# Batch normalisation over 64 tiles: stores moved to GpSimd's software queue in packets of eight rows, ScalarE computing most tiles

## The chip, the cores and the metric

One core of a Trainium2 chip runs the kernel. The metric is the device time of one execution in microseconds (us), the median over runs. A profile of one execution gives a span, from the first to the last instruction, and a record of each instruction and of each DMA packet.

## The reference

The input `x` has 32 images of 256 channels of 128 x 128 float32 values; each channel has a `gamma`, a `beta`, a running mean and a running variance. The result has the shape of `x`:

```python
mean = running_mean.reshape(1, -1, 1, 1)
var = running_var.reshape(1, -1, 1, 1)
return gamma * (x - mean) / np.sqrt(var + 1e-5) + beta
```

With `scale = gamma / sqrt(var + eps)` and `shift = beta - mean * scale`, every value needs one multiplication and one addition. 536.9 MB are read and 536.9 MB are written.

## The kernel before

The work is 64 tiles: an image's 256 channels are two blocks of 128, one channel on each partition, and a tile is 128 partitions of 16384 values (64 KB a row, 8.4 MB in all). Three buffers (`NBUF`) hold tiles; tile i lies in buffer i % 3, is computed in place and stored from there. Buffers are handed on by semaphores, which are written out by hand: `loaded[s]` and `stored[s]` count a buffer's loads and stores (16 for each DMA), `vdone` and `adone` count the parts done by VectorE and ScalarE.

At the start, SyncE (SP) issues the left half of tile 0, then the four small parameter loads, then the right half of tile 0. VectorE turns the parameters so that each partition has its channel's values, and works out `scale_t` and `shift_t`, with one square root on ScalarE.

Then the engines run over the tiles, each with an instruction order of its own.

- SP (L104) issues the load of tile i when the store of tile i - 3 is complete (L103), and also not before VectorE has done its first part of tile i - 1: a wait on `vdone` against 2 (i - 1) + 1. So one load is under way at a time.
- VectorE (`vector_part`, L132) computes columns 0 to 2560 (`STEP`) of a tile when it has landed, and then columns 2560 to 14336 (`VCOLS`).
- ScalarE (`scalar_part`, L143) computes the last 2048 columns. It waits for VectorE's two parts and, from tile 1 on, for the store of tile i - 1. Then it issues the store of tile i from its own queue (`store`, L156).
- The last tile is split anew: VectorE does 9216 columns (`VLAST`), ScalarE 7168 beside it.

At the end SP waits for all stores. `step` only chains the small parameter instructions to one another. GpSimd has no work but four small constants.

Of the kernel before, what the change touches and what calls it, by code (L numbers as in the profile page):

```python
# [7 lines left out]

NBUF = 3
PAD = 936  # L10


STEP = 2560
VCOLS = 14336
VLAST = 9216


@with_exitstack
def kernel(
    ctx: ExitStack,  # L20
    tc: tile.TileContext,
    x: bass.AP,
    gamma: bass.AP,
    beta: bass.AP,
    running_mean: bass.AP,
    running_var: bass.AP,
    out: bass.AP,
):
    nc = tc.nc
    eps = 1e-5  # L30
    f32 = mybir.dt.float32

    N, C, H, W = x.shape
    P = nc.NUM_PARTITIONS
    assert C % P == 0
    NCB = C // P
    HW = H * W
    NT = N * NCB
    B = 32
    NQ = P // B  # L40
    NE = 16
    NPAR = 4

    xr = x.rearrange("n (cb p) h w -> (n cb) p (h w)", p=P)
    outr = out.rearrange("n (cb p) h w -> (n cb) p (h w)", p=P)

    params = ctx.enter_context(tc.tile_pool(name="params", bufs=1))
    data = ctx.enter_context(tc.tile_pool(name="data", bufs=1))
    params.tile([P, PAD], f32, name="pad", tag="pad")
    bufs = [data.tile([P, HW], f32, name=f"t{s}", tag=f"t{s}") for s in range(NBUF)]  # L50
    rows = params.tile([B, NPAR * C], f32, name="rows", tag="rows")
    turned = params.tile([B, NPAR * C], f32, name="turned", tag="turned")
    par = params.tile([P, NPAR, NCB], f32, name="par", tag="par")
    eps_t = params.tile([P, 1], f32, name="eps_t", tag="eps")
    std_t = params.tile([P, NCB], f32, name="std_t", tag="std")
    rstd_t = params.tile([P, NCB], f32, name="rstd_t", tag="rstd")
    scale_t = params.tile([P, NCB], f32, name="scale_t", tag="scale")
    ms_t = params.tile([P, NCB], f32, name="ms_t", tag="ms")
    shift_t = params.tile([P, NCB], f32, name="shift_t", tag="shift")

    loaded = [tc.alloc_semaphore(f"loaded{s}") for s in range(NBUF)]
    stored = [tc.alloc_semaphore(f"stored{s}") for s in range(NBUF)]
    early = tc.alloc_semaphore("early")
    vdone = tc.alloc_semaphore("vdone")
    adone = tc.alloc_semaphore("adone")
    fetched = tc.alloc_semaphore("fetched")
    vec = tc.alloc_semaphore("vec")
    act = tc.alloc_semaphore("act")  # L70

    with tc.tile_critical():  # L72
        count = [0]

        def step(inst, sem=None, value=None):

            if sem is not None:
                inst._wait_ge(sem, value)
            elif count[0]:
                inst._wait_ge(vec, count[0])  # L80
            inst.then_inc(vec, 1)
            count[0] += 1
            return count[0]

        left, right = slice(0, HW // 2), slice(HW // 2, HW)
        last = NT - 1

        nc.sync.dma_start(out=bufs[0][:, left], in_=xr[0][:, left]).then_inc(early, 16)  # L90
        zeroed = step(nc.vector.memset(rows[:], 0.0))  # L91
        for r, ap in enumerate((running_var, gamma, beta, running_mean)):
            inst = nc.sync.dma_start(out=rows[0:NE, r * C : (r + 1) * C], in_=ap.partition_broadcast(NE))  # L93
            if r == 0:
                inst._wait_ge(vec, zeroed)
            inst.then_inc(fetched, 16)
        nc.sync.dma_start(out=bufs[0][:, right], in_=xr[0][:, right]).then_inc(loaded[0], 16)
        for i in range(1, NT):
            s, turn = i % NBUF, i // NBUF


            if turn:
                nc.sync.wait_ge(stored[s], 16 * turn)  # L103
            inst = nc.sync.dma_start(out=bufs[s][:], in_=xr[i]).then_inc(loaded[s], 16)  # L104
            if turn:
                inst._wait_ge(vdone, 2 * (i - 1) + 1)


        step(nc.vector.memset(eps_t[:], eps))  # L109
        step(nc.vector.transpose(out=turned[:], in_=rows[:]), fetched, 16 * NPAR)  # L110

        blocks = turned.rearrange("p (rc q b) -> p rc q b", q=NQ, b=B)
        flat = par.rearrange("p r cb -> p (r cb)")
        for q in range(NQ):
            placed = step(nc.vector.tensor_copy(out=flat[q * B : (q + 1) * B], in_=blocks[:, :, q, 0]))  # L115
        var_t, gamma_t, beta_t, mean_t = (par[:, r] for r in range(NPAR))
        nc.scalar.activation(  # L117
            out=std_t[:],
            in_=var_t,
            func=mybir.ActivationFunctionType.Sqrt,  # L120
            bias=eps_t[:],
            scale=1.0,
        )._wait_ge(vec, placed).then_inc(act, 1)
        step(nc.vector.reciprocal(out=rstd_t[:], in_=std_t[:]), act, 1)  # L124
        step(nc.vector.tensor_mul(out=scale_t[:], in0=gamma_t, in1=rstd_t[:]))  # L125
        step(nc.vector.tensor_mul(out=ms_t[:], in0=mean_t, in1=scale_t[:]))  # L126
        ready = step(nc.vector.tensor_sub(out=shift_t[:], in0=beta_t, in1=ms_t[:]))  # L127
        nc.vector.wait_ge(vec, ready)

        def vector_part(i, first, end):  # L130
            t, cb = bufs[i % NBUF], i % NCB
            return nc.vector.tensor_scalar(  # L132
                out=t[:, first:end],
                in0=t[:, first:end],
                scalar1=scale_t[:, cb : cb + 1],
                scalar2=shift_t[:, cb : cb + 1],
                op0=mybir.AluOpType.mult,
                op1=mybir.AluOpType.add,
            ).then_inc(vdone, 1)

        def scalar_part(i, first):
            t, cb = bufs[i % NBUF], i % NCB
            return nc.scalar.activation(  # L143
                out=t[:, first:],
                in_=t[:, first:],
                func=mybir.ActivationFunctionType.Identity,
                bias=shift_t[:, cb : cb + 1],
                scale=scale_t[:, cb : cb + 1],
            ).then_inc(adone, 1)

        def landed(i):
            return loaded[i % NBUF], 16 * (i // NBUF + 1)

        def store(i):
            s = i % NBUF
            nc.scalar.dma_start(out=outr[i], in_=bufs[s][:])._wait_ge(adone, i + 1).then_inc(stored[s], 16)  # L156

        vector_part(0, 0, HW // 2)._wait_ge(early, 16)
        vector_part(0, HW // 2, VCOLS)._wait_ge(*landed(0))
        for i in range(1, NT):  # L160
            vector_part(i, 0, STEP)._wait_ge(*landed(i))
            vector_part(i, STEP, VLAST if i == last else VCOLS)
        for i in range(last):
            nc.scalar.wait_ge(vdone, 2 * (i + 1))
            inst = scalar_part(i, VCOLS)
            if i:
                inst._wait_ge(stored[(i - 1) % NBUF], 16 * ((i - 1) // NBUF + 1))
            store(i)
        scalar_part(last, VLAST)._wait_ge(*landed(last))
        nc.scalar.wait_ge(vdone, 2 * NT)  # L170
        store(last)

        for s in range(NBUF):
            nc.sync.wait_ge(stored[s], 16 * ((NT - s + NBUF - 1) // NBUF))
# [30 lines left out]
```

## Time and profile before

| | us |
|---|---|
| median of 3 runs (2482.81 to 2484.91) | 2482.82 |
| span of the profiled execution | 2481.0 |
| VectorE busy in it | 508.8 |
| ScalarE busy in it | 139.8 |
| median time from issue to landing, load | 37.0 |
| median time from issue to landing, store | 36.5 |

How the profile is read: "busy" is the time in which an engine executes instructions; issuing a DMA is not counted. The DMA queues have rows of their own, with packets, megabytes and the share of the time of the core's 16 DMA engines that their packets took. q1 is SP's queue, q10 is ScalarE's. A window's "DMA share" is the mean busy share of the 16 engines, with packets counted where they start; the clock in it is TensorE's, which does nothing here. A timeline row has the start, the duration, the engine, the line and the operation; SPq and ACTq are the issuing instructions of SP and ScalarE.

### The profile page before, as it was taken

What the parts mean: (1) busy time and instruction counts of PE and PEld (TensorE: products, weight loads), DVE (VectorE), ACT (ScalarE), POOL (GpSimd) and SP (SyncE); (2) the same over time, 40 slices, a digit from 0 to 9 for tenths busy, and PEclk for the clock granted to TensorE, in tenths of its full rate; (3) what the DMA queues carried; (4) which work ended last, traced back from release to release, by engine and by line L of the source; (5) the groups of instructions that cost most, each with busy time, mean ns of one, the idle gap of its engine ahead of it and who ended that gap; (6) DMA issues with size and microseconds to landing.
All of it is one profiled execution on the core that took longest, in us unless ns stands there. A gap on an engine that the chain in (4) does not pass through costs nothing.

```text
span 2481.0 us, 516 instructions
## 1 busy us (share of the span) xinstructions
DVE 508.8 (21%) x139; ACT 139.8 (6%) x66; POOL 0.2 (0%) x4
## 2 busy tenths in 40 slices
DVE  2122121221212212122121221212212122121120
ACT  0000000000000000000000000000000000000001
POOL 0000000000000000000000000000000000000000
DMA  9999999999999999999999999999999999999999
GB/s 411 435 440 428 433 440 432 430 440 432 430 440 437 427 438 436 428 437 436 432 433 438 430 434 437 432 432 437 434 431 436 437 428 437 437 428 435 437 432 402
DMA packets 18708, 1073.85 MB, mean 433 GB/s; under 512 B 2128, under 2 KB 2192, under 8 KB 2192
## 3 DMA queue, kind: packets, MB, share of 16 engines
q1 hardware_dynamic: 9488, 536.94, 50.0%
q10 hardware_dynamic: 9216, 536.88, 49.9%
q14 instruction: 4, 0.03, 0.0%
HBM read 536.94 MB, written 536.87 MB: 433 GB/s over the span
## 4 chain that ended last, share of the span: by engine, by line
DMA 92%; DVE 4%; another core or an unknown queue 2%; ACT 0%; issue 0%; SPq 0%; DVEq 0%
DMA t<-in_x_dram 92%; DVE t L132 4%; ACT t L143 0%; SPq L93 0%; DVE rows L91 0%; DVE eps_t L109 0%; DVEq L200 0%; SPq L72 0%
## 5 line engine op out<-in xcount | busy, mean ns | idle before, releaser
L132 DVE TENSOR_SCALAR t<-t,scale_t,shift_t 128x11776 f32<-128x11776 f32 (+2 forms) x128 | 505.3, 3989 | 1928.8 <-DMA t<-in_x_dram 1928.7
L143 ACT ACTIVATE t<-t,shift_t,scale_t 128x2048 f32<-128x2048 f32 x64 | 138.2, 2159 | 2297.8 <-DMA out_dram<-t 2274.9
L110 DVE STREAM_TRANSPOSE turned<-rows 32x1024 f32<-32x1024 f32 x1 | 1.2, 1232 | 11.8 <-DMA rows<-in_running_mean_dram 11.8
L117 ACT ACT_TABLE_LOAD x1 | 1.3, 1283 | 0.9 <-SPq L72 0.9
L91 DVE MEMSET rows<- 32x1024 f32 x1 | 0.9, 912 | 1.2 <-SPq L72 1.2
L117 ACT ACTIVATE std_t<-par,eps_t 128x2 f32<-128x2 f32 x1 | 0.3, 295 | 14.0 <-DVE par L115 14.0
L115 DVE COPY par<-turned 32x8 f32<-32x8 f32 x4 | 0.6, 162 | 0.1
L124 DVE RECIPROCAL rstd_t<-std_t 128x2 f32<-128x2 f32 x1 | 0.2, 166 | 0.4 <-ACT std_t L117 0.4
L125 DVE TENSOR_TENSOR scale_t<-par,rstd_t 128x2 f32<-128x2 f32 x1 | 0.2, 162 | 0.0
L127 DVE TENSOR_TENSOR shift_t<-par,ms_t 128x2 f32<-128x2 f32 x1 | 0.2, 162 | 0.0
L126 DVE TENSOR_TENSOR ms_t<-par,scale_t 128x2 f32<-128x2 f32 x1 | 0.2, 160 | 0.0
L189 POOL MEMSET const-bfloat16-1.0<- 128x1 bf16 x1 | 0.1, 101 | 0.0
L189 POOL MEMSET const-uint8-127<- 128x1 uint8 x1 | 0.1, 101 | 0.0
L189 POOL MEMSET const-float32-0.0<- 128x1 f32 x1 | 0.1, 98 | 0.2 <-issue 0.2
L189 POOL MEMSET const-float32-1.0<- 128x1 f32 x1 | 0.1, 98 | 0.0
L109 DVE MEMSET eps_t<- 128x1 f32 x1 | 0.1, 59 | 0.1
## 6 DMA issues: line engine op xcount, KB each, us to landing
t<-in_x_dram SPq DMA_DIRECT2D x2, 4096.0 KB, 15.9
out_dram<-t ACTq DMA_DIRECT2D x64, 36.5
t<-in_x_dram SPq DMA_DIRECT2D x63, 37.0
rows<-in_running_var_dram SPq DMA_DIRECT2D x1, 16.0 KB, 11.1
rows<-in_gamma_dram SPq DMA_DIRECT2D x1, 16.0 KB, 10.9
rows<-in_beta_dram SPq DMA_DIRECT2D x1, 16.0 KB, 10.7
rows<-in_running_mean_dram SPq DMA_DIRECT2D x1, 16.0 KB, 10.6
```

What stands on the lines that cost most here:

```text
L91: zeroed = step(nc.vector.memset(rows[:], 0.0))
L109: step(nc.vector.memset(eps_t[:], eps))
L110: step(nc.vector.transpose(out=turned[:], in_=rows[:]), fetched, 16 * NPAR)
L115: placed = step(nc.vector.tensor_copy(out=flat[q * B : (q + 1) * B], in_=blocks[:, :, q, 0]))
L117: nc.scalar.activation(out=std_t[:], in_=var_t, func=mybir.ActivationFunctionType.Sqrt, bias=eps_t[:], scale=1.0,)._wait_ge(vec, placed).t ...
L124: step(nc.vector.reciprocal(out=rstd_t[:], in_=std_t[:]), act, 1)
L125: step(nc.vector.tensor_mul(out=scale_t[:], in0=gamma_t, in1=rstd_t[:]))
L126: step(nc.vector.tensor_mul(out=ms_t[:], in0=mean_t, in1=scale_t[:]))
L127: ready = step(nc.vector.tensor_sub(out=shift_t[:], in0=beta_t, in1=ms_t[:]))
L132: return nc.vector.tensor_scalar(out=t[:, first:end], in0=t[:, first:end], scalar1=scale_t[:, cb : cb + 1], scalar2=shift_t[:, cb : cb + 1 ...
L143: return nc.scalar.activation(out=t[:, first:], in_=t[:, first:], func=mybir.ActivationFunctionType.Identity, bias=shift_t[:, cb : cb + 1] ...
L189: nc = _bacc.Bacc("TRN2", target_bir_lowering=False, num_devices=1)
```

## The change

Stores are issued by GpSimd with `single_packet=True`, in tile order, each when ScalarE has counted its tile in `adone` (and for the first and the last tile when VectorE has done its part). The 128 rows of a store are spread over 16 DMA engines, eight rows in one packet for each. Loads stay on SP's queue: the first three are issued at once with semaphores of their own (`first`), and each later one waits for its buffer's store alone. ScalarE computes tiles 1 to 62 whole, one instruction of 16384 columns each; VectorE keeps the first half of tile 0 and 9216 columns of the last tile. ScalarE's wait for the previous store is gone, as is the load's wait for VectorE.

```diff
-STEP = 2560
-VCOLS = 14336
+NHEAD = 3
 VLAST = 9216
...
+    first = [tc.alloc_semaphore(f"first{s}") for s in range(NHEAD)]
...
-        nc.sync.dma_start(out=bufs[0][:, right], in_=xr[0][:, right]).then_inc(loaded[0], 16)
-        for i in range(1, NT):
-            s, turn = i % NBUF, i // NBUF
-            if turn:
-                nc.sync.wait_ge(stored[s], 16 * turn)
-            inst = nc.sync.dma_start(out=bufs[s][:], in_=xr[i]).then_inc(loaded[s], 16)
-            if turn:
-                inst._wait_ge(vdone, 2 * (i - 1) + 1)
+        nc.sync.dma_start(out=bufs[0][:, right], in_=xr[0][:, right]).then_inc(first[0], 16)
+        for i in range(1, NHEAD):
+            nc.sync.dma_start(out=bufs[i][:], in_=xr[i]).then_inc(first[i], 16)
+
+        def landed(i):
+            if i < NHEAD:
+                return first[i], 16
+            s = i % NBUF
+            before = 1 if s < NHEAD else 0
+            return loaded[s], 16 * (i // NBUF + 1 - before)
...
         nc.vector.wait_ge(vec, ready)
+        nc.scalar.wait_ge(vec, ready)
...
-        def landed(i):
-            return loaded[i % NBUF], 16 * (i // NBUF + 1)
-
-        def store(i):
+        vector_part(0, 0, HW // 2)._wait_ge(early, 16)
+        vector_part(last, 0, VLAST)._wait_ge(*landed(last))
+        scalar_part(0, HW // 2)._wait_ge(*landed(0))
+        for i in range(1, last):
+            scalar_part(i, 0)._wait_ge(*landed(i))
+        scalar_part(last, VLAST)._wait_ge(*landed(last))
+
+        for i in range(NHEAD, NT):
             s = i % NBUF
-            nc.scalar.dma_start(out=outr[i], in_=bufs[s][:])._wait_ge(adone, i + 1).then_inc(stored[s], 16)
-
-        vector_part(0, 0, HW // 2)._wait_ge(early, 16)
-        vector_part(0, HW // 2, VCOLS)._wait_ge(*landed(0))
-        for i in range(1, NT):
-            vector_part(i, 0, STEP)._wait_ge(*landed(i))
-            vector_part(i, STEP, VLAST if i == last else VCOLS)
-        for i in range(last):
-            nc.scalar.wait_ge(vdone, 2 * (i + 1))
-            inst = scalar_part(i, VCOLS)
-            if i:
-                inst._wait_ge(stored[(i - 1) % NBUF], 16 * ((i - 1) // NBUF + 1))
-            store(i)
-        scalar_part(last, VLAST)._wait_ge(*landed(last))
-        nc.scalar.wait_ge(vdone, 2 * NT)
-        store(last)
+            inst = nc.sync.dma_start(out=bufs[s][:], in_=xr[i])
+            if i >= NBUF:
+                inst._wait_ge(stored[s], 16 * (i // NBUF))
+            inst.then_inc(loaded[s], 16)
+        for i in range(NT):
+            if i in (0, last):
+                nc.gpsimd.wait_ge(vdone, 1 if i == 0 else 2)
+            nc.gpsimd.dma_start(out=outr[i], in_=bufs[i % NBUF][:], single_packet=True)._wait_ge(adone, i + 1).then_inc(
+                stored[i % NBUF], 16
+            )
```

## The prediction

> **What bounds the kernel now.** I read the page first: its queues, its busy times, its DMA issues.
>
> ```profile
> span 2481.0 us, 516 instructions
> DVE 508.8 (21%) x139; ACT 139.8 (6%) x66; POOL 0.2 (0%) x4
> ...
> q1 hardware_dynamic: 9488, 536.94, 50.0%
> q10 hardware_dynamic: 9216, 536.88, 49.9%
> ...
> out_dram<-t ACTq DMA_DIRECT2D x64, 36.5
> t<-in_x_dram SPq DMA_DIRECT2D x63, 37.0
> ```
>
> The two queues, loads (q1) and stores (q10), fill 50.0 + 49.9% of the time of the 16 DMA engines. VectorE is busy for 21%, ScalarE for 6%. So the bound is the time that packets take on the DMA engines, and a compute edit counts only where those engines run dry. Next, stretches of eight packet times (19.31 us, so that whole packets are counted), to see whether the mix of reads and writes matters.
>
> ```profile
> core 0: us, DVE busy (x) ACT busy (x) POOL busy (x), PEclk, DMA share, GB/s
> 2452.40:2471.71 19.31, 0.00 (x0) 0.00 (x1) 0.00 (x0) 1.00 1.00 434
> 34.00:53.31 19.31, 0.00 (x0) 0.00 (x0) 0.00 (x0) 1.00 1.00 434
> 1000.00:1386.24 386.24, 79.36 (x20) 20.93 (x10) 0.00 (x0) 1.00 1.00 434
> ...
> 5.00:24.31 19.31, 7.96 (x11) 0.29 (x1) 0.00 (x0) 1.00 1.02 433
> ```
>
> Row by row: stores alone 434 GB/s, loads and stores in turn 434, ten tiles of the middle 434, loads alone 433 (with the small parameter loads among them). The mix does not matter. The packet records say the same: a row of 64 KB takes 2418 ns in either queue, and one engine starts the next 2414 ns after the last; a packet of 32 KB takes 1213 ns. So 32 KB more cost 1205 ns, 64 KB cost 2410, and about 4 ns a packet are lost between packets. A tile is 8 rows on each engine, 8 x 2.414 = 19.3 us; load and store together 38.6 us, which is the spacing of the store issues (1003.58, 1042.18). The last view is the end of the timeline.
>
> ```profile
> 2433.65 0.34 ACTq L156 DMA_DIRECT2D out_dram<-t  x1
> 2446.04 6.36 ACT L143 ACTIVATE t<-t,shift_t,scale_t 128x7168 f32<-128x7168 f32 x1 [12.42 <-DMA t<-in_x_dram]
> 2446.04 5.27 DVE L132 TENSOR_SCALAR t<-t,scale_t,shift_t 128x2560 f32<-128x2560 f32 x2 [31.21 <-DMA t<-in_x_dram]
> 2452.43 0.34 ACTq L156 DMA_DIRECT2D out_dram<-t  x1
> ```
>
> The last tile lands at 2446.04 and takes 6.36 us of compute. The engines don't idle meanwhile: store 62, issued at 2433.65, is still being moved, and by the packet records store 63 follows it without a gap. That cover is what I watch below.
>
> **The change, part by part.** All sums are on the profiled execution: span 2481.0, of which the engines move data from 1.95 to 2479.36 (packet records). The median of the runs, 2482.82, lies 1.8 above the span; I add that at the end.
>
> *Compute.* ScalarE takes whole tiles. From the two widths in the groups, 2048 columns in 2092 ns and 7168 in 6362, a column costs 0.834 ns, so 16384 cost 2.09 + 14336 x 0.000834 = 14.05 us. 62 of them are 871 us, a third of the span, under 38.6 us of DMA time per tile. VectorE loses 126 of its 128 instructions; none was on the path. Price zero while the engines have other packets; the 14.05 us count only for when a store becomes ready. Tile 0's second half, 8192 columns, costs 2.09 + 6144 x 0.000834 = 7.2 us on ScalarE instead of 3.48 + 2.09 on both, so store 0 is some 2 us later, and with GpSimd's issue 4: hidden, for loads 1 and 2 (2 x 19.3 us from 23.4 on) are queued from the start.
>
> *Loads without the two gates.* Load i now waits for its slot's store alone, no longer for the previous tile's first vector step, and ScalarE's tiles no longer wait for the previous store. With three slots, one is loading, one is computed and stored, one is queued to load. Slot k is free again about 0.4 (landing to compute) + 14.05 + 2 (issue) + up to 5 (turn) + 19.3 + 2 = 43 us after load k landed; it is needed when load k+2 has ended, 77 us after. So 34 us are in hand, and the load queue never runs dry in the middle. Gain zero too, since the engines are already full at 434 GB/s.
>
> *Packets of eight rows.* 128 rows over 16 engines are 8 per engine. If the 4 ns are lost per packet, 7 x 4.2 ns x 64 stores = 1.9 us are saved; if they are lost per row, nothing. I take 1.9, since 32 KB and 64 KB packets carry the same excess over size. The engine takes turns between queues by packet: in the records of the middle, q1 and q10 alternate. So a store will hold its engine for 19.3 us while loads stand still, then loads run alone. By the windows neither direction alone is slower.
>
> *GpSimd issues the stores.* No GpSimd DMA is in this trace, so issue to first data is bounded by the nearest rows: the first load of all moves 1.0 us after its issue on SP; a store on ScalarE's queue at 1003.58, which had to await its turn, 3.5. [...]
>
> *What queues behind what.* GpSimd has nothing but stores on it, so a store that waits for ScalarE holds up only later stores. SP's next load waits for a store's completion with the 34 us in hand. A load's completion mark is a packet of its own and can be caught behind a store's 19.3 us packet; that delays ScalarE, again inside the 34 us.
>
> *The end.* Store 62 is ready 0.4 + 14.05 + 2.0 = 16.5 us after load 62 landed. Load 63 began when load 62 ended and has then done 6 to 7 of its 8 packets on each engine. The records show that a store waits 2.5 to 4.6 us more for its turn (3.5 to 5.6 us from issue, less the 1.0), so it starts 19.0 to 21.1 us after: about when the eighth packet is due. On whichever engine the store goes first, load 63's end, or its completion mark, comes only after the store. Then load 63 lands when store 62 is already over. Nothing is left to move while tile 63 is computed: 0.4 from the last data to compute, 6.36 of compute, 2.0 for GpSimd's issue: 8.8 us with idle DMA engines, where before there were none. Bounds: with 1.0 and 3.5 for the issue, 7.8 to 10.3.
>
> **Sum:** 2481.0 - 1.9 + 8.8 = 2487.9 span; with 1.8, **2489.7 us**. With the bounds, 2488.7 (or 2486.8 if GpSimd had no delay at all) to 2493.1 (no packet saving, late issue).
>
> [...]
>
> **The rivals.**
> 1. *The end stays covered.* If store 62 comes after load 63 has wholly ended, tile 63 is computed under it, and no engine idles. It decides at about 19.3 us from landing to the store's start on all engines, and I put that start at 19.0 to 21.1. But a store that misses load k+1 then runs in a pair with store k+1, and tile 63 must be the second of its pair; with tile 0 alone (its half tile is ready early) pairs are 1-2 to 61-62, and 63 is left over. For: the turn is close. Against: this parity. Time 2481.0 - 1.9 + 1.8 = 2480.9, no change. Chance 0.11.
> 2. *The packet stays one row.* If the flag does nothing here, loads and stores alternate as before, store 62 is stretched over 38.6 us and covers the end as it does now: 2482.8, no change. 9216 packets in the store queue would show it. Chance 0.11.
> 3. *The software queue is slower.* Each 1% on the stores is 64 x 19.3 x 0.01 = 12.4 us, undisguised, as the engines are the bound. The nearest bad row: the packets around the first store (28 to 34 us) took 2830 ns on average instead of 2418, once, 0.8 us per engine. If each store's start cost that, 64 x 0.8 = 51 us. In the middle none does. With 1% and the open end: 2502; with the 51 us, 2541. Chance 0.14.
> 4. *Faster.* At 2410 ns a row throughout, 1024 rows an engine need 2467.8; with 1.95 ahead and 1.6 behind the span is 2471.4, the time 2473.2. To gain over 5 us, half of what lies above that floor must go, and the 1.9 of the packets is not enough; the rest would have to come from the slow packets of the first 34 us (0.8 + 0.8 us per engine) and the 0.5 spread over later ones, with the end covered. Time about 2477. Chance 0.12.
>
> **How the numbers follow.** The forecast's case has 0.52. What a measurement can tell from no change is 0.2%, 5 us: 2477.9 to 2487.8. Of the forecast's case some 0.44 lies above 2487.8 and 0.08 below. Slower: 0.44 + 0.14 = 0.58. Same: 0.08 + 0.11 + 0.11 = 0.30. Faster 0.12. The range: below 2479 lies the fourth rival, 0.12; above 2500 more than half of the third, 0.08; so 2479 to 2500. The forecast's case alone is 2487 to 2493.
>
> **What would show it.** Right: a store queue of some 2048 packets (1024 of 512 KB and the marks); ScalarE tiles of 14.05 us; store issues 38.6 us apart on average; stores landing in about 25 us (2 + 3.5 for the turn + 19.3) instead of 36.5 and loads, issued early, in about 73 (3 x 38.6 - 43) instead of 37.0; after the last load lands, 8 to 9 us with no packets, then 19.3 us of store 63 alone. Wrong: DMA engines idle elsewhere, a stores-only stretch clearly under 434 GB/s, engines that end far apart, or store 62 still moving while tile 63 is computed.

## The result, and the profile after

Over 20 runs each, the changed kernel took 2495.57 us in the median (2485.83 to 2519.09), the kernel before 2483.8 (2482.39 to 2487.68): a ratio of 1.006, 95% interval 1.0039 to 1.008. It is slower by 0.6%. The median says less than the list: 9 of the 20 executions lie at 2485.8 to 2487.0, the other 11 anywhere from 2493.8 to 2519.1. The kernel before has no such second kind. I call them the low and the late executions. The profile below is of a low one (span 2484.1).

First its page: busy times, queues, issues to landing.

```profile
span 2484.1 us, 272 instructions
DVE 13.1 (1%) x13; ACT 885.6 (36%) x66; POOL 34.4 (1%) x68
...
q1 hardware_dynamic: 9488, 536.94, 49.9%
q0 software_dynamic: 9216, 536.88, 49.9%
...
out_dram<-t POOLq DMA_DIRECT2D x64, 46.3
t<-in_x_dram SPq DMA_DIRECT2D x63, 55.2
```

q0 is GpSimd's queue. It has 9216 packets, exactly as many as q10 had before: 8192 rows of 64 KB and 1024 completion marks. In the packet records of the middle the queues take turns on an engine after one row, at times two, so nothing held an engine for eight rows: the packets of eight rows that the title and the change speak of did not come about. Stores take 46.3 us to land, loads 55.2, for both queues now have work at nearly all times.

The windows of the same run: the middle, then the last tile's compute, then what follows the last row.

```profile
core 0: us, DVE busy (x) ACT busy (x) POOL busy (x), PEclk, DMA share, GB/s
1000.00:1386.24 386.24, 0.00 (x0) 140.40 (x10) 5.33 (x10) 1.00 1.00 434
2448.50:2455.20 6.70, 5.08 (x1) 6.36 (x1) 0.00 (x0) 1.00 0.90 391
...
2477.30:2484.10 6.80, 0.00 (x0) 0.00 (x0) 0.00 (x0) 1.00 0.00 1
```

The middle is as full as before, 434 GB/s. While the last tile is computed the engines are 90% busy: store 62 is still being moved. But 6.8 us pass after the last row, where the kernel before needed 1.6 (2479.36 to 2481.0). SP's own waits name the cause.

```profile
SPq L158 <- DMA out_dram<-t: 2367.0, 61, 69.4
...
SPq L70 <- POOLq L70: 5.1, 1, 5.1
```

When all stores have landed, SP waits 5.1 us for GpSimd. The instruction records have it as a DRAIN on GpSimd at the end of the block, 5292 ns long. So a low execution sums up as 2481.0 + 5.2 (end) - 2.1 (the last row ends at 2477.27 instead of 2479.36) = 2484.1. Of the 2.1, some 1.4 us per engine come from the end, where the engines finish within 0.6 us of one another instead of 2.6, and 0.6 from fewer slow rows.

### The profile page after: what moved, and what is told of

Its sections match the earlier page's. It is cut to its first block, busy times and chain, and to the rows that moved or that the text cites. A ratio compares the mean times of both kernels' runs of the same rounds, so it can differ in the third digit from the quotient of the medians.

```text
span 2484.1 us, 272 instructions
## 1 busy us (share of the span) xinstructions
DVE 13.1 (1%) x13; ACT 885.6 (36%) x66; POOL 34.4 (1%) x68
## 3 DMA queue, kind: packets, MB, share of 16 engines
q0 software_dynamic: 9216, 536.88, 49.9%
## 4 chain that ended last, share of the span: by engine, by line
another core or an unknown queue 61%; ACT 35%; DMA 2%; issue 0%; SPq 0%; DVE 0%; POOL 0%; DVEq 0%
ACT t L139 35%; DMA t<-in_x_dram 2%; SPq L89 0%; DVE rows L87 0%; POOL out_dram L165 0%; SPq L93 0%; DVE eps_t L105 0%; DVEq L196 0%; SPq L70 0%
## 5 line engine op out<-in xcount | busy, mean ns | idle before, releaser
L139 ACT ACTIVATE t<-t,shift_t,scale_t 128x16384 f32<-128x16384 f32 (+1 forms) x64 | 884.0, 13813 | 1554.3 <-DMA t<-in_x_dram 1554.3
L165 POOL DMA_DIRECT2D out_dram<-t x64 | 34.2, 535 | 2421.1 <-ACT t L139 2421.1
L128 DVE TENSOR_SCALAR t<-t,scale_t,shift_t 128x8192 f32<-128x8192 f32 (+1 forms) x2 | 9.6, 4813 | 2426.7 <-DMA t<-in_x_dram 2426.5
## 6 DMA issues: line engine op xcount, KB each, us to landing
out_dram<-t POOLq DMA_DIRECT2D x64, 46.3
t<-in_x_dram SPq DMA_DIRECT2D x63, 55.2
```

What stands on the lines that cost most here:

```text
L128: return nc.vector.tensor_scalar(out=t[:, first_col:end], in0=t[:, first_col:end], scalar1=scale_t[:, cb : cb + 1], scalar2=shift_t[:, cb ...
L139: return nc.scalar.activation(out=t[:, first_col:], in_=t[:, first_col:], func=mybir.ActivationFunctionType.Identity, bias=shift_t[:, cb : ...
L165: nc.gpsimd.dma_start(out=outr[i], in_=bufs[i % NBUF][:], single_packet=True)._wait_ge(adone, i + 1).then_inc(stored[i % NBUF], 16)
```

## The experiments

**1. The late executions, and what the flag does.** The changed kernel again, and the changed kernel without its flag:

```diff
-            nc.gpsimd.dma_start(out=outr[i], in_=bufs[i % NBUF][:], single_packet=True)._wait_ge(adone, i + 1).then_inc(
+            nc.gpsimd.dma_start(out=outr[i], in_=bufs[i % NBUF][:])._wait_ge(adone, i + 1).then_inc(
```

> The changed kernel as it is, to see whether one chip shows both kinds of execution: 9 of its 20 runs lay at 2485.8 to 2487.0 us, 11 between 2493.8 and 2519.1, and the profile is of the lowest. Theory A (the software queue has good and bad executions): both kinds among these runs, and a profile above 2490 us shows packets of over 2418 ns or gaps in the store queue. Theory B (the loads without gates slip into another order in some executions): both kinds too, but the packets stay at 2418 ns and the excess is time in which engines have no packet.

> The changed kernel with single_packet left out. The profile of the changed kernel shows 8192 store packets of 64 KB that take turns with the loads row by row, so by it the flag does nothing: 9216 store packets again, the same 5 us of GpSimd at the end, a span of about 2484 in the best execution, and the same spread. If the flag does act in a way the records do not show, and it makes the spread, all runs lie near 2486.

Both kinds showed in each, on one chip. e1_after_again: 6 of 12 runs at 2485.9 to 2486.3, 6 at 2499.5 to 2512.1. e2_no_flag: 5 of 12 at 2485.8 to 2486.7, 7 at 2496.8 to 2523.2; its queue has the same 9216 packets and its drain the same 5292 ns. So the flag does nothing that a packet count, a duration or a time shows.

The profile of e1_after_again caught a late execution. Its windows, an early stretch, a later one, and the compute of the last tile:

```profile
core 0 of [0], span 2510.4 us
...
300.00:1000.00 700.00, 0.00 (x0) 253.22 (x19) 9.59 (x18) 1.00 1.00 434
1200.00:2400.00 1200.00, 0.00 (x0) 424.41 (x31) 15.99 (x30) 1.00 1.00 429
2474.90:2484.00 9.10, 5.08 (x1) 6.36 (x1) 0.53 (x1) 1.00 0.39 166
```

It starts like a low one at 434 GB/s and falls to 429 after 1200 us, with the engines busy throughout (share 1.00): packets take longer. While tile 63 is computed the share is 0.39: here most engines have run out of work, the idle end that the prediction had put into every execution. By the packet records the last row ends 26.3 us later than in the low execution. What rows of 64 KB take beyond 2418 ns, called slow rows from here on, makes 18.2 us per engine instead of 0.7, and idle time 9.5 instead of 0.9. The two differences, 17.5 and 8.6, are nearly all of it. The idle time lies at the end: 9.2 us of it in the last 40 us before the last row ends, against 0.3 in the low execution. So this late execution is slow rows for two thirds and the open end for one third. Both queues have slow rows (11.0 us per engine in stores, 7.2 in loads). Theory A had expected them in the store queue, theory B no slow rows at all: neither was right on that.

**2. Software queue or missing gates?** Two kernels, each with one of the two. e3_act_queue is the changed kernel with its stores on ScalarE's hardware queue; e4_before_gpsimd is the kernel before with its stores on GpSimd:

```diff
 # e3_act_queue, against the changed kernel
             scalar_part(i, 0)._wait_ge(*landed(i))
+            nc.scalar.dma_start(out=outr[i], in_=bufs[i % NBUF][:])._wait_ge(adone, i + 1).then_inc(
+                stored[i % NBUF], 16
+            )
 ...
-            nc.gpsimd.dma_start(out=outr[i], in_=bufs[i % NBUF][:], single_packet=True) ...
 # e4_before_gpsimd, against the kernel before
-            nc.scalar.dma_start(out=outr[i], in_=bufs[s][:])._wait_ge(adone, i + 1).then_inc(stored[s], 16)
+            nc.gpsimd.dma_start(out=outr[i], in_=bufs[s][:], single_packet=True)._wait_ge(adone, i + 1).then_inc(stored[s], 16)
 ...
-        nc.scalar.wait_ge(vdone, 2 * NT)
+        nc.gpsimd.wait_ge(vdone, 2 * NT)
```

> The changed kernel with the stores on ScalarE's hardware queue, each right behind its tile's instruction; GpSimd issues nothing. It keeps the loads without gates and ScalarE's whole tiles. Theory A (everything comes from the software queue): no end of 5 us, no spread, 2480 to 2483 us in all runs, 0 to 3 below the kernel before. Theory B (the loads without gates make the spread): best runs at 2480 to 2483, others 8 to 33 us above.

> The kernel before with its stores issued by GpSimd with single_packet, all gates and VectorE's share kept. Theory A (software queue): 5 us more than before at the end in every run, 2488 us at best, and the spread of the changed kernel. Theory B (loads without gates): 2488 in all runs and no spread. [...]

This pair separates them. e3_act_queue has both kinds, 5 of 12 runs at 2481.0 to 2484.3 and 7 at 2492.9 to 2513.8, without any GpSimd DMA. e4_before_gpsimd has one kind, 2487.1 to 2489.9 in 11 runs; ratio to the kernel before 1.002 (1.0012 to 1.0029). So the late executions belong to the loads and tiles without gates, not to the software queue, which costs little but its drain: 5.6 us by the medians (2489.03 against 2483.42 on the same chip). The two kernels also differ in who computes the tiles; experiment 4 comes back to that. The page of e3_act_queue, a low execution:

```profile
span 2479.3 us, 269 instructions
...
q1 hardware_dynamic: 9488, 536.94, 50.0%
q10 hardware_dynamic: 9216, 536.88, 50.0%
```

At 2479.3 its span is 4.8 below the changed kernel's: the drain is gone, the even finish of the engines is kept. In e4_before_gpsimd stores take 36.2 us to land, against 36.5 on ScalarE's queue: neither VectorE's work nor GpSimd's issue costs anything here that can be seen.

**3. What the drain depends on.** Four kernels, each the kernel before with some work for GpSimd; `kept(i)` is the semaphore and count of store i, as software and hardware stores have semaphores of their own here:

```diff
 # e7_gpsimd_memset                # e8_gpsimd_one_dma: a 16 KB load on GpSimd in its place, awaited by SP at the end
+        nc.gpsimd.memset(spare[:], 0.0)
 # e9_last_on_gpsimd: soft(i) is i == NT - 1;  e10_first32_gpsimd: i < 32
+            queue = nc.gpsimd if soft(i) else nc.scalar
-            nc.scalar.dma_start(out=outr[i], in_=bufs[s][:])._wait_ge(adone, i + 1).then_inc(stored[s], 16)
+            queue.dma_start(out=outr[i], in_=bufs[s][:])._wait_ge(adone, i + 1).then_inc(kept(i)[0], 16)
 ... (the other waits on stored[...] become waits on kept(...))
```

> The kernel before plus one memset of 32 x 256 on GpSimd at the start, no DMA of GpSimd's: GpSimd then takes part in the drain at the end of the block. If the 5.3 us drain comes with any work of GpSimd: span 2486, time 2488. If it comes with the software queue: as before, 2482 to 2485.

> The kernel before plus one small load (16 KB) issued by GpSimd at the start, of data that nothing uses. If the drain at the end comes with the software queue, however little it moved: GpSimd's drain takes 5.3 us after the last store, span 2486, time 2488. If it grows with the 64 stores: under 1 us more than before.

> The kernel before with only the last store on GpSimd. One small GpSimd load at the start left a drain of 0.13 us, 64 stores one of 5.29. If the drain comes with a software DMA late in the kernel: 5.3 us again, span 2486. If it grows with the number of software DMAs: under 0.3 us, span 2481 to 2483.

> The kernel before with the first 32 stores on GpSimd, the rest on ScalarE's queue. If the drain grows with the number: about 2.7 us. If it comes with a software DMA late in the kernel: 0.1 us, as none is near the end. If it comes with any stores of that size: 5.3 us.

GpSimd's drain took 41 ns with the memset, 125 with the one load, 135 with the last store, 2669 with the first 32 stores, 5292 with 64. In these kernels it grows with the number of software DMAs, not with their bytes (a load of 16 KB and a store of 8.4 MB differ by 10 ns): (2669 - 135) / 31 = 82 ns for each from one DMA to 32, (5292 - 2669) / 32 = 82 ns for each from 32 to 64. The wait of SP in e10_first32_gpsimd, where GpSimd had issued nothing for the second half:

```profile
SPq L82 <- POOLq L82: 2.5, 1, 2.5
```

e7 and e8 are not to be told from the kernel before (ratios 1.0001, 0.9992 to 1.001, and 1.0004, 0.9994 to 1.0013). e9 and e10 ran once each (2483.56 and 2487.21 us), so for them the drain's own record counts and not the time. The last store on GpSimd in e9 landed 27.1 us after its issue, the same store on ScalarE's queue in the kernel before 27.3.

**4. Which gate.** One gate put back into e3_act_queue, and one gate taken from the kernel before:

```diff
 # e5_load_gate, against e3_act_queue
+            nc.sync.wait_ge(*landed(i - 1))
             inst = nc.sync.dma_start(out=bufs[s][:], in_=xr[i])
 # e6_store_gate, against e3_act_queue
+            nc.scalar.wait_ge(stored[(i - 1) % NBUF], 16 * ((i - 1) // NBUF + 1))
             scalar_part(i, 0)._wait_ge(*landed(i))
 # e11_before_no_load_gate, against the kernel before
-            if turn:
-                inst._wait_ge(vdone, 2 * (i - 1) + 1)
 # e12_before_no_store_gate, against the kernel before
-            if i:
-                inst._wait_ge(stored[(i - 1) % NBUF], 16 * ((i - 1) // NBUF + 1))
```

> The kernel with stores on ScalarE's hardware queue and ScalarE computing whole tiles (e3_act_queue), plus one gate: load i is issued only when load i - 1 has landed. Theory C (the engines fall out of step because a queue holds more than one load, and a load gate puts them in step again each tile): all runs at 2481 to 2484 us, none above 2488. Theory D (the store side sets it: stores of two tiles in flight): half of the runs 10 to 33 us above, as without the gate.

> The same kernel (e3_act_queue) with the other gate alone: ScalarE starts tile i only when the store of tile i - 1 is complete; loads as slots come free. Theory C (load gate): the spread stays, best runs 2481, others up to 2515. Theory D (store gate): all runs within 3 us. In both the engines stay busy in the middle, since a load or a store is always queued.

> The kernel before without the load gate (the wait on VectorE's first part of the previous tile); all else kept. Theory C (several loads in the queue let the engines fall out of step): a spread of 10 to 30 us above a best of 2481 to 2483. If the store gate alone keeps order: all runs within 5 us.

> The kernel before without the store gate (ScalarE's wait for the previous store); the load gate kept. Theory C: no spread, all runs within 5 us of 2483. If both gates are needed: a spread as large as the changed kernel's.

Measured, in us; the last two columns are per engine, from the packet records of each run's profile, and "slow rows" is again the time beyond 2418 ns:

| kernel | runs | last row ends | slow rows | idle |
|---|---|---|---|---|
| before (both gates) | 2482.0 to 2487.7 | 2479.4 | 1.3 | 2.4 |
| e11: store gate only | 2720.4 to 2729.7 | 2725.8 | 103.8 | 146.0 |
| e12: load gate only | 2553.1 to 2556.5 | 2551.5 | 61.7 | 14.0 |
| e3: no gate, whole tiles, low execution | 2481.0 to 2513.8 | 2477.1 | 0.7 | 0.6 |
| e5: e3 with a load gate | 2488.2 to 2492.6 | 2486.6 | 8.6 | 2.1 |
| e6: e3 with the store gate | 2728.3 to 2731.0 | 2727.0 | 114.0 | 137.2 |

I had forecast none of the large numbers; three of the four expectations were out by 70 to 250 us, and e5's by 4 to 8. In each row the added slow rows and idle time make up the distance from the kernel it was made from (e11: 102.5 + 143.6 = 246.1, against 246.4).

No kernel with a gate shows the two kinds in its 4 to 11 runs. e5 is the closest test: whole tiles on ScalarE as in e3_act_queue, one gate more, and its 6 runs lie within 4.4 us. So whole tiles alone do not make the late executions; a load gate ends them, but at 4 to 8 us above the level that had been expected. Two things stay untested here: e5 ran on another chip than e3_act_queue, and the kernel before was not tried with its own split of the tiles and neither gate.

How e11 loses its time can be read off. Its timeline, two of its windows and the wait of its loads; then, for comparison, the kernel before around the issue of a store (1003.58) and of a load (1017.59):

```profile
1018.66 7.93 DVE L130 TENSOR_SCALAR t<-t,scale_t,shift_t 128x2560 f32<-128x2560 f32 x2 [34.39 <-DMA t<-in_x_dram]
1021.06 84.77 SPq L104 DMA_DIRECT2D t<-in_x_dram  x3
1021.06 2.10 ACT L141 ACTIVATE t<-t,shift_t,scale_t 128x2048 f32<-128x2048 f32 x1 [40.24 <-DMA out_dram<-t]
1023.19 0.34 ACTq L154 DMA_DIRECT2D out_dram<-t  x1
```

```profile
core 0: us, DVE busy (x) ACT busy (x) POOL busy (x), PEclk, DMA share, GB/s
1017.00:1024.00 7.00, 5.34 (x2) 2.10 (x1) 0.00 (x0) 1.00 0.80 300
1024.00:1060.00 36.00, 2.59 (x1) 0.00 (x0) 0.00 (x0) 1.00 0.99 421
```

```profile
SPq L104 <- DMA out_dram<-t: 2615.0, 61, 67.0
```

```profile
core 0: us, DVE busy (x) ACT busy (x) POOL busy (x), PEclk, DMA share, GB/s
1001.00:1008.00 7.00, 0.00 (x0) 2.09 (x1) 0.00 (x0) 1.00 1.04 449
1015.00:1022.00 7.00, 6.05 (x2) 0.00 (x0) 0.00 (x0) 1.00 1.01 440
```

A load has landed at 1018.66, and at 1021.06 the store before it completes, which releases the next load and ScalarE's part at once. Load and store then set out together, take turns for 36 us and end together; both queues are empty at the same moment, and each of the 62 periods (42.1 us by the next issue) loses 143.6 / 62 = 2.3 us of idle time and 1.7 us in the first rows after it. The loads wait 2615.0 us in all, 42.9 each, for a store: tiles have landed one ahead, so the slot that a load needs is the one being stored. In the kernel before the engines are full at both issues. e6_store_gate gets there in another way: store i cannot be issued before 14.05 us of compute after store i - 1 has landed, and issue to landing is 28.3, so a period is 42.4 us instead of 38.6, whatever the loads do.

```profile
ACT t L139 <- DMA out_dram<-t: 1786.1, 62, 44.3
```

Those are ScalarE's waits in e6_store_gate, 28.8 us a tile, all on stores. So the two gates of the kernel before are a pair: together they keep a load's issue 14.0 us behind the store's (1017.59 and 1003.58 in the kernel before), so that one queue covers the other's gap; without the load gate 246 us are lost in the profiled execution, without the store gate 72. How the 72 us of e12 come about was not tested. The time between the two issues may matter: the store follows a load's issue by 8.5 us in e12 (1012.41 and 1020.87) and by 14.0 in e5 (2341.52 and 2355.55), which also has only a load gate and loses 9 us, not 72. Without both gates the low execution is tighter than with them (idle 0.6 instead of 2.4), but more than half of the executions are late.

## Why the prediction was right or wrong, point by point

The direction and the range held, and 0.6% is close to the forecast 0.3%. The mechanism did not hold, and the closeness is luck: the forecast added -1.9 and +8.8 us, a low execution is +5.2 - 2.1, the median over both kinds 11.8 above the kernel before. No low execution has the end that the forecast priced at 8.8 us, as far as profiled; the one late execution that was profiled has it. The two other costs that the runs show, the drain and the slow rows, were priced at nothing. One bound was also added up wrongly: without any delay of GpSimd the time by the forecast's own terms is 2489.7 - 2.0 = 2487.7, not 2486.8.

- *What bounds the kernel*, and that reads, writes and their mix go at one rate: right for before (433 and 434 GB/s in its windows); the mix in the middle of the low execution after has 434 GB/s.
- *Compute*: right. A whole tile takes 14.04 us (14.05 forecast), and the engines stay full over it in the profiled low execution.
- *Packets of eight rows*, -1.9 us: wrong, zero. The packet stays one row and the queues take turns by row, which was the condition of the second rival. I took the flag at its word; the order of the rows and the count of 9216 are the evidence. In the low executions with and without the flag an engine switches queues after one row, at times two, while both queues have work.
- *The end*, +8.8 us: wrong in the low execution (engines 90% busy during tile 63's compute), since it followed from the eight-row packet. In the late execution of e1_after_again most engines do idle there (share 0.39), and the idle time at the end is 9.2 us against 0.3, nearly the 8.8 that were forecast. But there is no eight-row packet in it either: its engines had come out of step, with some 12 of them done with store 62 while 4 still moved it. The size is right there by chance.
- *GpSimd issues the stores*, 2.0 us once: wrong in kind. No run shows the 2.0 us by itself: in the profiled low execution store 63's first rows start 2.14 to 2.75 us after its issue, just as store 62's last rows end (packet records), and issue to landing is as on ScalarE's queue (36.2 against 36.5 under the gates). What costs is the drain, 82 ns a store and 5.3 us in all, behind the last landing where nothing hides it. No row of the kernel before shows it, as GpSimd issues no DMA there, and I had weighed only a cost at the issue.
- *Loads without the two gates*, zero: this is the step that failed most. The 34 us in hand were worked out with stores that land in about 25 us and taken to hold for every order of loads and stores. In the low execution stores land in 46.3 us and loads 55.2 after their issue, 16.6 more than the 38.6 of a tile, so about half of the 34 is left, which is enough. But full queues were not the whole condition: more than half of the executions take 8 to 33 us more, and in the one of them that was profiled rows become slow although loads still wait in the queue (58.3 us from issue to landing), and the end is open. And in e11 the three slots are not enough at all, as each load waits for the store of its slot.
- *The third rival*, a slower software queue: not so. In the low execution store rows take 2418 ns from the 5th to the 95th percentile, and all 16 engines end within 0.6 us of one another. But the price that I set aside in it, slow rows when a store sets out after a stretch of loads, is part of what the late execution pays.

**What stays open** is why rows become slow. In the late execution 12 engines start a store row within 0.9 us (1435.6 to 1436.4), just after all 16 had loaded, and those rows take 3.2 to 3.9 us; 13 such moments make 9.6 of its 18.2 us per engine. Yet the kernel before changes from 15 or 16 loading engines to at most 2 within 1 us some 55 times, and loses nothing there. A sharp change of direction is thus not enough, and no run shows what else it takes. Nor was it tried what first makes an execution a late one. Only one late execution was profiled.

## What to carry to other kernels

Here loads and stores shared full DMA engines (434 GB/s in the middle), and a wait that looked idle, the load gate, kept the two queues from running empty together: with that gate alone left out, 246 us were lost in the profiled execution (e11_before_no_load_gate). Where a kernel has such gates, try each one's removal alone and all of them together, with many runs each, and read the whole list of times, not a best one or a single profile. The 64 stores on GpSimd's software queue brought a bill of 5.3 us after the last landing, 32 of them one of 2.7 (e10_first32_gpsimd), so the end is worth a look too, and not the issue alone.

## What was not expected of the hardware

GpSimd's drain at the end of the block took 41 ns without a software DMA in it, 125 with one load, 2669 with 32 stores and 5292 with 64, 82 ns for each beyond the first, and the 2669 came although the last of the 32 had been issued half the kernel earlier (e10_first32_gpsimd). With both queues empty at the same moment, the first two load rows afterwards took 2.7 to 3.8 us instead of 2.42 on all engines (e11_before_no_load_gate, from 1022 us on). And executions of one DMA-bound program on one chip differed by 26 us (e1_after_again) and 37 us (e2_no_flag).
